# Splitting the 512-column product matmuls of a hybrid decoder layer into two of 256 columns

## The chip, the cores and the metric

One core of a Trainium2 chip runs the whole kernel. The metric is the device time of one execution in microseconds (us). Three runs of the kernel before took 1301.55, 1302.9 and 1303.37 us; the median is 1302.9 us.

## What is computed

One decoder layer over 1024 positions of width 1024, in float32. A single projection of the normed input feeds two branches, a chunked state-space scan (Mamba-2) and an attention with a forget gate; their outputs are projected, gated, added and projected again:

```python
def _hybrid_layer(x, ...):
    h = _rmsnorm(x, pre_g)
    proj = jnp.einsum('bld,de->ble', h, w_in)          # 1024 -> 9248 columns
    z_ssm, xbc, dt_raw, q, k, v, f_raw, z_att, g_ssm, g_att = jnp.split(proj, ...)
    xbc = jax.nn.silu(_causal_dwconv(xbc, conv_w, conv_b))
    y = _ssd_chunked(...)                              # 16 heads of 64, chunks of 128
    ...                                                # gate by silu(z_ssm), group norm
    o = _forgetting_attention(heads(q), heads(k), heads(v), log_f)
    y_att = o * jax.nn.silu(z_att)
    p_ssm = jnp.einsum('ble,ed->bld', y_ssm, w_branch_ssm)
    p_att = jnp.einsum('ble,ed->bld', y_att, w_branch_att)
    merged = jax.nn.sigmoid(g_ssm) * p_ssm + jax.nn.sigmoid(g_att) * p_att
    out = jnp.einsum('bld,de->ble', merged, w_out)
    return x + _rmsnorm(out, post_g)
```

## The kernel before

All the large matrix products (the projection, the two branch projections and the output projection) go through one class, `Pair`. A pair holds two blocks of 128 output columns, and multiplies them with the 1024 positions by a scheme of seven products in place of eight: the sums of the weight blocks (`total`, line 357) are made on VectorE or GpSimd, the sums of the other operand are made once for many pairs, and each of the seven products covers 512 of the 1024 inputs and 512 positions. There are 48 pairs, so 336 products.

Each number is held as a high part and a low part of a reduced float32 type (`fp32r` in the profile's forms of the writers, f32 in those of the readers). `Pair.split` (lines 351 and 352) makes both parts of the weights in the tile `wop`, one on ScalarE and one on VectorE; the other operand's parts are the tiles x0h, x0l to x6h, x6l. A product is the sum of three part products, high by high, high by low and low by high, over four blocks of 128 inputs (`KH` = 4): twelve matmuls of 128 weight columns by 512 positions (`HALF` = 512), in `Pair.matmuls`. They accumulate in one bank of PSUM, and are recorded through the helper `mm`, so that all of them have line 130 in the profile. The bank's tile is called pb, pc or pd.

`Pair.do` says which products go to which bank. Products 1, 2 and 5 open a bank (`first` is true, and the first of their twelve matmuls clears it); products 6, 7, 4 and 3 go on adding to a bank that is open. After a product the bank is copied out by `keep` (ScalarE, line 404, tile s) or combined with an earlier copy by `give` (lines 412 to 418, tiles th, u and others).

`Stream` holds the list of all products in the order in which they are done. A call of `half` issues half a product (six matmuls, up to the `yield`), and the code of the branches calls it between its own steps: the scan (`ssd`), attention (`scores`, `turned`, `weighted`), the norms. So TensorE's program alternates between pieces of products and pieces of the branches, and TensorE's order is written by hand (`mm` and `turn` keep the program order). Other instructions that are not pinned are put in order by the scheduler, which goes by a simulated clock of its own.

Attention works on pairs of heads. Its scores (tile s) are matmuls of 64 rows, two of them side by side on the two halves of the array, over 128 to 512 positions, with the high and low parts of the same reduced type. ScalarE's exponential (line 1468, tile ex) follows, then transposes by TensorE (`turn`, line 133, tile pt), a copy (line 1499, tile p), and the weighting of the values (tile av). Eight pairs of heads with six groups each make 48 groups, and in each group two stretches of products are issued (`fill`), one after the scores and one after the transposes.

Of the kernel before, what the change touches and what calls it, by code (L numbers as in the profile page):

```python
# [20 lines left out]
KH = NK // 2  # L21
NT = T // P
HALF = 512
# [63 lines left out]
def hybrid_layer(ctx: ExitStack, tc, a, out):  # L87
# [41 lines left out]
    def mm(*args, **kw):  # L129
        return tc.keep_in_program_order(nc.tensor.matmul(*args, **kw))  # L130
# [191 lines left out]
    class Pair:  # L322
# [65 lines left out]
        def matmuls(self, ps, which, x, first):  # L388

            op = self.op.pop(which)  # L390
            xh, xl = self.ops[x]
            for k in range(KH):
                if k == KH // 2:
                    yield
                for n, (w, m) in enumerate(((0, xh), (0, xl), (1, xh))):
                    mm(
                        ps, op[:, w, k, :], m[:, k, :], start=first and k == 0 and n == 0,
                        stop=k == KH - 1 and n == 2, skip_group_check=True,
                    )

        def keep(self, ps):
            s = wp.tile([P, HALF], F32, tag="s", bufs=3, name="s")
# [890 lines left out]
    with tc.tile_pool(name="att", bufs=1, reuse_waits="tile", side="right") as ap, tc.tile_pool(  # L1293
# [24 lines left out]
        q, k, v, fb = {}, {}, {}, {}  # L1318
# [408 lines left out]
```

## Time and profile before

| | |
|---|---|
| median of three runs | 1302.9 us |
| profiled execution, first to last instruction (the only time that its page gives) | 1304.1 us |
| TensorE matmuls | 7054, busy 1259.0 us |
| TensorE weight loads | 7054, busy 984.6 us |
| VectorE | busy 1009.6 us |
| ScalarE | busy 791.9 us |
| GpSimd | busy 263.9 us |
| mean granted TensorE clock | 0.996 |
| HBM traffic | 180 GB/s over the span |

In the profile's rows PE is TensorE's matmul part and PEld its weight loads; DVE is VectorE, ACT is ScalarE, POOL is GpSimd, SP is the engine whose queue issues most transfers. A row of the timeline has the start, the length, the engine, the line of the kernel, the operation, the tile written and the tiles read, the shapes, and how many neighbouring instructions it stands for. Matmuls overlap: the length of one is longer than the distance to the next, and the ends are modelled. A row of groups has the count, then the busy time and the mean length of one in ns, then the idle time before it with what ended that.

### The profile page before, as it was taken

What the parts mean: (1) busy time and instruction counts of PE and PEld (TensorE: products, weight loads), DVE (VectorE), ACT (ScalarE), POOL (GpSimd) and SP (SyncE); (2) the same over time, 40 slices, a digit from 0 to 9 for tenths busy, and PEclk for the clock granted to TensorE, in tenths of its full rate; (3) what the DMA queues carried; (4) which work ended last, traced back from release to release, by engine and by line L of the source; (5) the groups of instructions that cost most, each with busy time, mean ns of one, the idle gap of its engine ahead of it and who ended that gap; (6) DMA issues with size and microseconds to landing.
All of it is one profiled execution on the core that took longest, in us unless ns stands there. A gap on an engine that the chain in (4) does not pass through costs nothing.

```text
span 1304.1 us, 20960 instructions
## 1 busy us (share of the span) xinstructions
PE 1259.0 (97%) x7054; PEld 984.6 (76%) x7054; DVE 1009.6 (77%) x1994; ACT 791.9 (61%) x1738; POOL 263.9 (20%) x250
## 2 busy tenths in 40 slices
PE   5999999999999999999999999999999999899997
PEld 4678878777888888788877777777667777678886
DVE  7989986887888888898767566666787676686975
ACT  7745665456665666567545666666675657653754
POOL 3000440013400340124101021120001002146052
PEclk9999999999999999999999999999999999899999
DMA  8222543555436543654365575666866658556933
GB/s 294 76 107 75 164 143 100 161 170 172 130 110 199 175 145 96 209 164 137 114 207 198 183 227 190 225 211 217 281 206 241 211 194 295 190 170 201 364 107 104
DMA packets 153515, 233.57 MB, mean 179 GB/s; under 512 B 15968, under 2 KB 61504, under 8 KB 153408
## 3 DMA queue, kind: packets, MB, share of 16 engines
q1 hardware_dynamic: 142016, 205.53, 49.4%
q0 software_dynamic: 4864, 15.99, 3.1%
q10 hardware_dynamic: 6528, 10.72, 2.2%
q8 instruction: 55, 0.90, 0.3%
q14 instruction: 52, 0.43, 0.1%
HBM read 162.99 MB, written 72.34 MB: 180 GB/s over the span
## 4 chain that ended last, share of the span: by engine, by line
PE 66%; DVE 12%; ACT 8%; DMA 7%; issue 4%; POOL 1%; SPq 1%; ACTq 0%; DVEq 0%; POOLq 0%
PE pb L130 27%; PE pc L130 16%; PE av L130 5%; PE pd L130 4%; PE pt L133 4%; PE s L130 4%; ACT ex L1468 2%; DVE wop L352 2%; PE yps L130 2%; DMA raw<-in_wu 1%; DMA qh_dram<-th 1%; DVE sum L357 1%; ACT wop L351 1%; DMA xt<-in_x 1%; DVE ex L1464 1%
## 5 line engine op out<-in xcount | busy, mean ns | idle before, releaser
L1468 ACT ACTIVATE ex<-ex,nm 128x512 f32<-128x512 f32 (+1 forms) x192 | 116.0, 606 | 131.1 <-DVE nm L1464 129.7
L352 DVE TENSOR_TENSOR wop<-sum,wop 128x512 fp32r<-128x512 f32 x180 | 138.2, 768 | 57.3 <-ACT wop L351 55.8
L351 ACT ACTIVATE wop<-sum 128x512 fp32r<-128x512 f32 x180 | 112.3, 625 | 80.1 <-DVE sum L357 34.1
L404 ACT ACTIVATE s<-pb 128x512 f32<-128x512 f32 x144 | 85.0, 590 | 88.7 <-PE pb L130 85.8
L352 DVE TENSOR_TENSOR wop<-raw,wop 128x512 fp32r<-128x512 f32 x144 | 105.2, 732 | 42.7 <-ACT wop L351 41.4
L130 PE MATMUL pc<-x3h,wop 128*128 128x512 f32 x384 | 131.4, 400 | 4.1 <-DVE th L418 2.8
L130 PE MATMUL pc<-x2h,wop 128*128 128x512 f32 x384 | 130.6, 399 | 2.4 <-DVE th L416 1.9
L130 PE MATMUL pb<-x0h,wop 128*128 128x512 f32 x384 | 131.3, 399 | 0.0
L130 PE MATMUL pb<-x6h,wop 128*128 128x512 f32 x384 | 129.3, 395 | 1.3 <-ACT s L404 1.3
L130 PE MATMUL pb<-x5h,wop 128*128 128x512 f32 x384 | 129.3, 395 | 1.0 <-ACT s L404 1.0
L130 PE MATMUL pb<-x4h,wop 128*128 128x512 f32 x384 | 129.4, 395 | 0.0
L1464 DVE CUSTOM_DVE_ANT_0 ex<-s,fb 128x512 f32<-128x512 f32 (+1 forms) x192 | 95.7, 552 | 36.0 <-PE s L130 36.0
L351 ACT ACTIVATE wop<-raw 128x512 fp32r<-128x512 f32 x144 | 89.6, 623 | 13.7 <-PE pc L130 5.8
L130 PE MATMUL pd<-x1h,wop 128*128 128x512 f32 x288 | 96.3, 394 | 0.0
L130 PEld LDWEIGHTS pc<-x3h,wop 128*128 128x128 f32 x384 | 72.6, 189 | 23.0 <-issue 4.1
L130 PEld LDWEIGHTS pc<-x2h,wop 128*128 128x128 f32 x384 | 72.1, 188 | 20.7 <-DVE th L416 3.3
L130 PEld LDWEIGHTS pb<-x5h,wop 128*128 128x128 f32 x384 | 72.1, 188 | 18.3 <-ACT s L404 1.8
L130 PEld LDWEIGHTS pb<-x6h,wop 128*128 128x128 f32 x384 | 72.2, 188 | 17.8 <-ACT s L404 2.1
L130 PEld LDWEIGHTS pb<-x0h,wop 128*128 128x128 f32 x384 | 72.7, 189 | 16.2 <-issue 0.9
L133 PE MATMUL pt<-ident,ex 128*128 128x128 f32 x576 | 76.9, 277 | 7.9 <-ACT ex L1468 7.5
L130 PEld LDWEIGHTS pb<-x4h,wop 128*128 128x128 f32 x384 | 72.1, 188 | 16.0 <-issue 0.9
L133 PEld LDWEIGHTS pt<-ident,ex 128*128 128x128 f32 x576 | 65.9, 142 | 19.8 <-ACT ex L1468 13.8
(310 smaller groups left out, 2921.6 us busy)
## 6 DMA issues: line engine op xcount, KB each, us to landing
raw<-in_wu SPq DMA_DIRECT2D x128, 256.0 KB
csb<-cs_dram SPq DMA_DIRECT2D x32, 256.0 KB
fb<-f_dram SPq DMA_DIRECT2D x16, 512.0 KB
rb<-st_dram SPq DMA_DIRECT2D x48, 128.0 KB
wd<-in_wo SPq DMA_DIRECT2D x40, 128.0 KB
xt<-in_x SPq DMA_DIRECT2D x8, 512.0 KB
gs_dram<-th ACTq DMA_DIRECT2D x16, 256.0 KB
qh_dram<-th SPq DMA_DIRECT2D x16, 256.0 KB
```

Source lines behind the costliest of these rows:

```text
L130: return tc.keep_in_program_order(nc.tensor.matmul(*args, **kw))
L133: return tc.keep_in_program_order(nc.tensor.transpose(out_, in_, idn))
L351: nc.scalar.activation(op[:, 0], src, AF.Copy)
L352: nc.vector.tensor_tensor(op[:, 1], src, op[:, 0], ALU.subtract)
L357: self.adds.tensor_tensor(t, x, y, ALU.add)
L404: nc.scalar.activation(s, ps, AF.Copy)
L1464: nc.vector.tensor_tensor_reduce(o, s[e][:, 0:w], fb[hp, h][:, e, 0:w], 1.0, 3.0e38, ALU.add, ALU.min, nm)
L1468: pin(nc.scalar.activation(o, o, AF.Exp, scale=-1.0, bias=nm, accum_out=hd.at(hd.sm, i, h, e)))
```

## The change

In `Pair.matmuls`, only the matmul that opens a bank keeps its 512 columns. Every other one is issued as two, for the columns 0 to 255 and 256 to 511 of the same bank, with the same weights. The flags stay as they were; the flag that ends a product is now on both halves of its last matmul.

```diff
                 for n, (w, m) in enumerate(((0, xh), (0, xl), (1, xh))):
-                    mm(
-                        ps, op[:, w, k, :], m[:, k, :], start=first and k == 0 and n == 0,
-                        stop=k == KH - 1 and n == 2, skip_group_check=True,
-                    )
+                    begin = first and k == 0 and n == 0
+
+                    for cols in (slice(0, HALF),) if begin else (slice(0, HALF // 2), slice(HALF // 2, HALF)):
+                        mm(
+                            ps[:, cols], op[:, w, k, :], m[:, k, cols], start=begin,
+                            stop=k == KH - 1 and n == 2, skip_group_check=True,
+                        )
```

## The prediction

> **What bounds the kernel now.** I read the page's engine totals first, then its chain, then the list of waits, then single places of the timeline.
>
> ```profile
> span 1304.1 us, 20960 instructions
> PE 1259.0 (97%) x7054; PEld 984.6 (76%) x7054; DVE 1009.6 (77%) x1994; ACT 791.9 (61%) x1738; POOL 263.9 (20%) x250
> PE 66%; DVE 12%; ACT 8%; DMA 7%; issue 4%; POOL 1%; SPq 1%; ACTq 0%; DVEq 0%; POOLq 0%
> PE pb L130 27%; PE pc L130 16%; PE av L130 5%; PE pd L130 4%; PE pt L133 4%; PE s L130 4%; ACT ex L1468 2%; DVE wop L352 2%; PE yps L130 2%; DMA raw<-in_wu 1%; DMA qh_dram<-th 1%; DVE sum L357 1%; ACT wop L351 1%; DMA xt<-in_x 1%; DVE ex L1464 1%
> ```
>
> TensorE is busy for 97% of the span, and it has one weight load for each matmul: 7054 of both. The chain that ended last runs over PE for 66%; the products (tiles pb, pc and pd) alone make up 27 + 16 + 4 = 47%. A busy share says little where matmuls overlap in the array, so the next question is whether the products really stand back to back. They do, in the merged chain, in the timeline, and in the count by window:
>
> ```profile
> 112.40 8.16 PE pb L130 x36
> 1272.58 0.39 PE L130 MATMUL pb<-x0h,wop 128*128 128x512 f32 x1
> 1272.58 0.19 PEld L130 LDWEIGHTS pb<-x0l,wop 128*128 128x128 f32 x1
> 1275.30 0.39 PE L130 MATMUL pb<-x6h,wop 128*128 128x512 f32 x1
> 0.00:700.00 700.00, 580.86 (x2466) 458.77 (x2466) 153.03 (x208) 130.12 (x209) 1.00 0.48 153
> 700.00:1140.00 440.00, 234.34 (x912) 165.05 (x912) 55.68 (x77) 47.25 (x77) 0.99 0.66 217
> 1140.00:1304.10 164.10, 150.07 (x654) 122.30 (x654) 44.84 (x51) 31.60 (x51) 0.99 0.56 189
> ```
>
> The first row gives 8.16 / 36 = 0.2267 us from one 512-column matmul to the next. The rows at 1272.58 and 1275.30 stand twelve matmuls apart: 2.72 / 12 = 0.2267 again. A matmul's own length (0.39) is longer than this, because neighbours overlap; what counts is the spacing. The load of the next matmul's weights starts when the matmul before starts (both at 1272.58) and takes 0.19, so it lies wholly beside the stream of 0.2267. The last three rows are the windows view for the tile wop alone (PE busy and count, then the loads): 2466 + 912 + 654 = 4032 product matmuls, so 4032 x 0.2267 = 914 us, or 70% of the span, are products.
>
> What TensorE waits for is little:
>
> ```profile
> PE pt L133 <- DVE rstd L1165: 8.6, 1, 8.6
> PE pt L133 <- ACT ex L1468: 7.5, 17, 1.3
> PE av L130 <- ACT p L1499: 4.5, 8, 1.2
> PE pc L130 <- DVE th L418: 3.3, 4, 1.5
> PE pb L130 <- ACT s L404: 2.3, 3, 1.3
> 1296.83 0.39 PE L130 MATMUL pb<-x6h,wop 128*128 128x512 f32 x1
> ```
>
> Idle in all is 1304.1 - 1259.0 = 45.1 us. Of it 8.6 come before the first transpose, and the last matmul ends at 1297.2, which leaves 6.9 after it. Between them 45.1 - 8.6 - 6.9 = 29.6 us are left over the whole kernel. So the kernel is bound by TensorE nearly everywhere, and a longer product is paid for nearly in full.
>
> **The change, part by part.** Of the 4032 product matmuls, the first of a bank stays whole: products 1, 2 and 5 open a bank, once for each of 48 pairs, so 144 matmuls. The other 3888 become two each: 3888 more matmuls, and as many more weight loads. The streamed columns stay the same. Will the second load really be issued, where the weights are the same as the first's? The kernel has such neighbours already: xh and xl are multiplied in turn by the same weights, and each xl matmul has a load of its own:
>
> ```profile
> L130 PE MATMUL pb<-x0l,wop 128*128 128x512 f32 x192 | 75.4, 393 | 0.0
> L130 PEld LDWEIGHTS pb<-x0l,wop 128*128 128x128 f32 x192 | 36.4, 190 | 6.8
> ```
>
> 192 matmuls and 192 loads: none is left out. Now the price of a half. No 256-column product stands in the trace; the nearest are the attention scores at 256 columns, which have the same number type for the moving side and 128 weight columns, but work on 64 rows each, two at a time in the two halves of the array:
>
> ```profile
> L130 PEld LDWEIGHTS s<-k,q 64*128 64x128 f32 x576 | 45.5, 185 | 15.3 <-issue 11.5 <-DMA fb<-f_dram 0.2 <-DMA th<-gs_dram 0.2
> 715.23 0.40 PE L130 MATMUL s<-k,q 64*128 64x256 f32 x4
> 715.35 0.28 PE L130 MATMUL s<-k,q 64*128 64x256 f32 x2
> ...
> 1141.90 0.39 PE L130 MATMUL s<-k,q 64*128 64x256 f32 x4
> 1142.02 0.28 PE L130 MATMUL s<-k,q 64*128 64x256 f32 x2
> 802.52 0.19 PEld L130 LDWEIGHTS pc<-x2h,wop 128*128 128x128 f32 x1
> 802.63 0.19 PEld L130 LDWEIGHTS pc<-x2l,wop 128*128 128x128 f32 x1
> ```
>
> From the second pair of scores to the third it is 0.12 at 715.23 and at 1141.90; these are the first and the last of 16 such places, which lie between 0.116 and 0.119 with a mean of 0.118. The last two rows are two loads of full product weights with no stream between: the second starts 0.11 after the first, though each is drawn 0.19 long. So a load holds the array for about 0.11, just under the 0.118, and still hides. I take 0.118 for a half. Two halves are 0.236 against 0.2267: 0.0093 more for each matmul that is split, and 3888 x 0.0093 = 36 us. Bounds: at 0.116 it is 0.0053 each, or 21 us; at 0.120 (a little above what the scores show, for the full-height load) it is 0.0133, or 52 us.
>
> The Trainium skill, "TensorE: Matmul & The Clock Gate", section "The mechanism" of Part 3, speaks against the change more strongly: it says that a weight load overlaps running matmuls only where it goes to another row group. By that rule each of the 3888 added loads would lie bare, at 0.11 each an estimated 428 us more. The trace disagrees already: the load at 1272.58 runs beside a matmul on the same rows.
>
> What of the 36 us is hidden? Only what falls into the 29.6 us of waits. Attention's 48 groups have two gaps each that are filled with products, and 912 products lie there: 9.5 a gap, which grow by 9.5 x 0.0093 = 0.09 us. The 25 waits on ex and p (17 and 8, of about 0.5 us each) can each swallow this much: 2.2 us. The waits on evicted sums (th and s, seven in the rows above) follow a chain of some 5 us, in which 22 products grow by 0.2 us: 1.4 us. I take 4 us hidden. Bounds: nothing, and the 29.6 whole.
>
> At no cost, with what covers it: the compiled kernels hold the same instructions on VectorE, ScalarE, GpSimd and the queues, but some neighbours change places (87 of 1996 on VectorE, 36 of 1594 on ScalarE, 19 of 874 on SP's queue, one of 252 on GpSimd), since the scheduler's own clock sees longer products. VectorE at 77% and ScalarE at 61% cover that; without the cover the waits on th and s (3.3 + 2.3) could double or go, so 6 us either way. No wait is added: the second half of the last matmul releases the bank, and the evictions queue as before. The added instructions have to be fetched and issued; the scores issue two loads and two matmuls in 0.118, twice what a half needs. The granted clock is the last term:
>
> ```profile
> 1100.00:1200.00 100.00, 93.08 (x493) 71.13 (x492) 71.55 (x141) 52.77 (x121) 36.27 (x28) 0.97 0.59 192
> ```
>
> 3% of these 100 us is a stretch at a lower clock in the last, half-empty attention groups; it may go or stay, 3 us at most.
>
> The sum: 1304.1 + 36 - 4 = 1336 for the profiled execution. Its span lies 1.2 us above the median of the three runs, so against these it is 1302.9 + 32 = 1335.
>
> **The rivals.** First, the loads stop hiding. If the whole drawn length of a load (189 ns for the products, by the rows of x0l and its like) had to pass between two starts, a half would cost 0.19 instead of 0.118: 3888 x (2 x 0.19 - 0.2267) = 596 us, so about 1900. It decides from the point where a load holds the array longer than 0.118. For it: a load of full height at the rate of a half has no example here. Against it: the scores' loads are drawn 185 ns long and follow each other every 0.118, and the product loads at 802.52 stand 0.11 apart.
>
> Second, the other side, faster: the time lost from one product matmul to the next belongs to the long stream and not to each instruction. The transposes of attention show a spacing with hardly any such time:
>
> ```profile
> 805.36 0.82 PE L133 MATMUL pt<-ident,ex 128*128 128x128 f32 x6
> L133 PE MATMUL pt<-ident,ex 128*128 128x128 f32 x576 | 76.9, 277 | 7.9 <-ACT ex L1468 7.5
> ```
>
> (0.82 - 0.277) / 5 = 0.109 for each. If a half-width product kept that beat, two would take 0.218, 0.0087 less than now: 3888 x 0.0087 = 34 us gained, so 1269. It decides from a half below 0.1134. For it: full-height matmuls with their loads do run at 0.109. Against it: those stream other data at 128 columns, and the scores, which are of the products' kind, need 0.118.
>
> Third, a small fixed time: a half costs 0.1146, so that a split costs some 2.5 ns, 10 us, and the time is 1313. For it: the scores come in pairs, and a second matmul issued beside the first may lengthen their beat, which a single product would not pay. Against it: none of the 16 places is below 0.116. The Trainium skill (same page, section "Back-to-back issue gap") gives the warm gap as the columns over 2.4 plus 2.5 ns; by it a split costs 2.5 ns and the estimate is 1313 too, but by it a 512-column matmul would take 216 ns, where the trace has 226.7.
>
> Fourth, TensorE is not the bound: the added time goes into its waits. At most 29.6 of the 36 us can, which leaves 1309; if the loads of the waiting matmuls hide there as well, no change at all is left.
>
> **How the numbers follow.** Forecast 0.86, loads bare 0.03, faster 0.04, small fixed time 0.04, hidden 0.03 (two thirds of it no change that can be measured). A measurement of this kernel tells about 0.2%, 2.6 us, from no change. That makes faster 0.04, same 0.02, slower 0.94. The range takes the bounds of the half: 1302.9 + 21 - 9 = 1315 (more hidden than I take, or a swap that helps), and 1302.9 + 52 + 3 = 1358 (nothing hidden, a stretch of low clock more). It leaves out the bare loads, the faster case, most of the hidden and the small fixed time, and some 0.06 of the forecast's own tails.
>
> **What would show it.** In the changed profile: 7054 + 3888 = 10942 matmuls and as many loads; product rows of 256 columns, with their starts 0.118 apart; stretches of twelve, now 2.72 us, that become 2.83 (twelve splits at 0.0093 more each; eleven where the stretch opens a bank); PE's share of the chain not lower than 66%; waits on ex and p a little shorter. A spacing of halves at 0.113 or less, or halves near 0.19, proves the forecast wrong at its main step. If the spacing is 0.118 and the time still stands within 3 us of before, then the waits hid it and the reading of the bound is wrong.

## The result and the profile after

The changed kernel takes 1342.5 us (median of 4 runs, 1341.96 to 1343.82) against 1303.1 us before: 39.4 us more, a ratio of 1.0295 with a 95% interval of 1.0274 to 1.0315. In a later set of runs it was 1341.5 against 1302.3, ratio 1.0307 (1.028 to 1.0334). The forecast was 1335 with a range of 1315 to 1358.

The page of the changed kernel, its span, engine totals and chain:

```profile
span 1340.3 us, 28752 instructions
PE 1300.6 (97%) x10942; PEld 1201.2 (90%) x10942; DVE 1011.2 (75%) x1994; ACT 793.8 (59%) x1738; POOL 256.6 (19%) x250
PE 76%; DVE 7%; ACT 6%; DMA 5%; issue 3%; POOL 1%; SPq 0%; ACTq 0%; DVEq 0%; POOLq 0%
PE pb L130 34%; PE pc L130 18%; PE pd L130 6%; PE av L130 4%; PE pt L133 4%; PE s L130 4%; ACT ex L1471 2%; PE yps L130 2%; DVE wop L352 1%; DMA raw<-in_wu 1%; DMA xt<-in_x 1%; PE tr L133 1%; ACT wop L351 1%; DVE ex L1467 1%; DVE sum L357 1%
```

TensorE has 10942 matmuls and as many loads, 3888 more of each. PE's share of the span stays at 97%, but that of the loads goes from 76% to 90%. PE's share of the chain goes up by ten points, and VectorE, ScalarE and the transfers lose nine between them: more of the chain now runs over TensorE. VectorE's busy time, 1011.2 us after 1009.6, has hardly moved, so its share falls with the longer span.

Now the beat of the products (the time from one start to the next): a long stretch of the merged chain, then a place in the timeline, then groups of one operand, the last of them from the trace before (a group's columns after the count are busy us, the mean length in ns, and the idle time before it):

```profile
69.29 8.63 PE pb L130 x71
```

```profile
115.20 0.64 PE L130 MATMUL pb<-x5h,wop 128*128 128x256 f32 x4
115.68 0.40 PE L130 MATMUL pb<-x5l,wop 128*128 128x256 f32 x2
115.92 0.64 PE L130 MATMUL pb<-x5h,wop 128*128 128x256 f32 x4
115.81 0.55 PEld L130 LDWEIGHTS pb<-x5h,wop 128*128 128x128 f32 x4
```

```profile
L130 PE MATMUL pc<-x2h,wop 128*128 128x256 f32 x768 | 134.6, 286 | 1.5 <-DVE th L419 1.3
L130 PEld LDWEIGHTS pc<-x2h,wop 128*128 128x128 f32 x768 | 109.1, 191 | 4.0 <-DVE th L419 1.9
```

```profile
L130 PEld LDWEIGHTS pc<-x2h,wop 128*128 128x128 f32 x384 | 72.1, 188 | 20.7 <-DVE th L416 3.3 <-issue 1.4 <-DVE u L416 0.8
```

Six halves fill the 0.72 us from 115.20 to 115.92: 0.120 each. The stretch of 71 is one opening matmul and 70 halves: 70 x 0.120 + 0.227 = 8.63. So a split matmul takes 0.240 where it took 0.2267. Over 3888 splits that is 51.7 us. The load path hardly rests any more: ahead of the 384 loads of x2h it was idle 20.7 us in all before, and ahead of the 768 of now it is idle 4.0 us.

Of these 51.7 us, 36.2 arrive in the two spans and 39.4 in the medians (the profiled execution of before was one of the slower ones). The waits of TensorE show a part of the rest:

```profile
PE pt L133 <- ACT ex L1471: 6.1, 15, 1.3
PE av L130 <- ACT p L1502: 4.8, 9, 1.0
PE pb L130 <- ACT s L407: 1.7, 2, 1.0
PE pc L130 <- DVE th L421: 0.8, 1, 0.8
```

The idle time of PE falls from 45.1 to 1340.3 - 1300.6 = 39.7 us. All start times of the two traces, set side by side, divide the 15.5 us that are missing between the spans. Delays of over 0.14 us beyond the beat, between one product matmul and the next, fall from 14.22 to 6.66 us in all (7.6 us). Waits among the transposes and other matmuls fall by 2.5 us. One half in five starts 0.116 to 0.118 and not 0.120 after its forerunner (4 us), and small irregularities get rarer (1.4 us).

### The profile page after: what moved, and what is told of

It reads as the page before. It is cut to its first block, busy times and chain, and to the rows that moved or that the text cites. A ratio compares the mean times of both kernels' runs of the same rounds, so it can differ in the third digit from the quotient of the medians.

```text
span 1340.3 us, 28752 instructions
## 1 busy us (share of the span) xinstructions
PE 1300.6 (97%) x10942; PEld 1201.2 (90%) x10942; DVE 1011.2 (75%) x1994; ACT 793.8 (59%) x1738; POOL 256.6 (19%) x250
## 4 chain that ended last, share of the span: by engine, by line
PE 76%; DVE 7%; ACT 6%; DMA 5%; issue 3%; POOL 1%; SPq 0%; ACTq 0%; DVEq 0%; POOLq 0%
PE pb L130 34%; PE pc L130 18%; PE pd L130 6%; PE av L130 4%; PE pt L133 4%; PE s L130 4%; ACT ex L1471 2%; PE yps L130 2%; DVE wop L352 1%; DMA raw<-in_wu 1%; DMA xt<-in_x 1%; PE tr L133 1%; ACT wop L351 1%; DVE ex L1467 1%; DVE sum L357 1%
## 5 line engine op out<-in xcount | busy, mean ns | idle before, releaser
L130 PE MATMUL pc<-x3h,wop 128*128 128x256 f32 (+1 forms) x720 | 135.1, 295 | 1.5 <-DVE th L421 0.8
L130 PE MATMUL pc<-x2h,wop 128*128 128x256 f32 x768 | 134.6, 286 | 1.5 <-DVE th L419 1.3
L130 PE MATMUL pb<-x0h,wop 128*128 128x256 f32 (+1 forms) x720 | 135.5, 295 | 0.0
L130 PE MATMUL pb<-x6h,wop 128*128 128x256 f32 x768 | 133.8, 285 | 1.0 <-ACT s L407 1.0
L130 PE MATMUL pb<-x5h,wop 128*128 128x256 f32 x768 | 133.7, 285 | 0.7 <-ACT s L407 0.7
L130 PE MATMUL pb<-x4h,wop 128*128 128x256 f32 x768 | 134.0, 285 | 0.0
L130 PEld LDWEIGHTS pb<-x6h,wop 128*128 128x128 f32 x768 | 109.7, 191 | 2.7 <-ACT s L407 1.4
L130 PEld LDWEIGHTS pb<-x4h,wop 128*128 128x128 f32 x768 | 109.5, 191 | 1.4 <-issue 0.9
L130 PE MATMUL pd<-x1h,wop 128*128 128x256 f32 (+1 forms) x540 | 99.6, 292 | 0.0
L130 PEld LDWEIGHTS pd<-x1h,wop 128*128 128x128 f32 x540 | 77.6, 190 | 3.5 <-issue 2.5
```

## The experiments

The forecast had two terms: what a split costs, and how much of it the waits swallow. The theories on the first:

- **Theory 1**: each matmul pays for its columns and a fixed time beside (13.3 ns, by 0.2267 and 0.120). This is the forecast's view.
- **Theory 2**: a half waits for its weight load; the 0.120 is the load's.

**Other widths.** Each operand is cut in its own way.

```diff
+WIDTHS = {
+    "b11": (0, 256, 512), "b21": (0, 384, 512), "-b22": (0, 448, 512), "t1": (0, 320, 512),
+    "-t2": (0, 128, 256, 384, 512), "t3": (0, 288, 512), "t4": (0, 512),
+}
 ...
-                    for cols in (slice(0, HALF),) if begin else (slice(0, HALF // 2), slice(HALF // 2, HALF)):
+                    edges = (0, HALF) if begin else WIDTHS[x]
+                    for lo, hi in zip(edges, edges[1:]):
+                        cols = slice(lo, hi)
```

> Each product is cut in its own way: x0 at 256, x1 at 384, x2 at 448, x3 at 320, x5 at 288, x4 into four of 128, x6 not at all. Theory 1 (every matmul pays its columns, 0.417 ns each, and a fixed 13.3 ns; that is what 0.2267 and 0.1200 for 512 and 256 columns give): starts 0.200 apart after 448 columns, 0.173 after 384, 0.147 after 320, 0.133 after 288, 0.107 after 224, 0.093 after 192, 0.067 after 128, 0.040 after 64; time about 1355. Theory 2 (the 0.120 of a half is the beat of the weight loads): the wide parts as in theory 1, but every part of 256 columns or fewer at 0.117 to 0.120; a pair of halves is then a lucky cut, the uneven ones cost up to 0.09 each, and the time is about 1303 + 250 = 1550.

Measured: 1521.7 us against 1303.4. In the timeline, the cut at 448 (x2), and then the quarters (x4) in the merged chain:

```profile
277.69 0.48 PE L134 MATMUL pc<-x2h,wop 128*128 128x448 f32 x2
278.00 0.48 PE L134 MATMUL pc<-x2l,wop 128*128 128x448 f32 x2
278.31 0.79 PE L134 MATMUL pc<-x2h,wop 128*128 128x448 f32 x4
278.94 0.45 PE L134 MATMUL pc<-x2l,wop 128*128 128x448 f32 x1
```

```profile
144.31 5.36 PE pb L134 x48
```

Four matmuls cut at 448 fill 1.25 us, 0.313 each; 48 quarters fill 5.36 us, 0.112 each. A part of 64 columns thus costs as much as one of 128. The medians of the starts, for one matmul of 512 columns that is cut:

| cut | 512 | 256 + 256 | 288 + 224 | 320 + 192 | 384 + 128 | 448 + 64 | 4 x 128 |
|---|---|---|---|---|---|---|---|
| us | 0.227 | 0.240 | 0.243 | 0.258 | 0.286 | 0.313 | 0.444 |

Theory 1 alone (0.240 for every cut in two) is dead. The narrow part costs what a load costs, about 0.111, and the sum of the wide part (at the 0.443 ns a column of 0.2267 for 512) and 0.111 meets each of the four uneven cuts within 6 ns. It misses the even cut by 16 ns: 0.113 + 0.111 is 0.224, not 0.240. Theory 2 holds for the narrow parts, but its figure was wrong: loads can follow each other every 0.111, below the 0.120 of a half. So this run leaves open what the 0.120 is. Single starts are not used here, only sums over a period: the gap after the 448 columns reads 0.284 and the one after the 64 reads 0.029. I take it that a matmul which waits for its load is drawn as started early.

**Other neighbours.** The part products are put in another order, so that three neighbours add to the same columns and few neighbours share their weights. (The expectation says that none do, but where one column half ends and the other begins, xl and xh still stand side by side on the high part of the weights: one neighbouring pair in six, where the changed kernel has four in six.)

```diff
-                for n, (w, m) in enumerate(((0, xh), (0, xl), (1, xh))):
-                    for cols in ...:                                 # shortened
+                for cols in (slice(0, HALF // 2), slice(HALF // 2, HALF)):
+                    for n, (w, m) in enumerate(((0, xh), (1, xh), (0, xl))):
 ...
```

> The same matmuls of 256 columns as the changed kernel, but the three part products of one column half come before the other half, with the two high-by-high and high-by-low ones apart, so that no two neighbours share their weights and three neighbours add to the same columns. Theories 1 and 2: spacing 0.120 as before, time as the changed kernel, 1342 within 4. Rival (the second half's load is cheaper because the weights stand there already, or neighbours on other columns of the bank are cheaper): spacing above 0.120, each ns worth 7.8 us.

Measured: 1343.2 us, the median spacing 0.120 for every operand. The stretch of three products in the merged chain is as long as in the changed kernel:

```profile
69.04 8.63 PE pb L130 x71
```

The rival is dead: far fewer loads find their weights there already, and nothing gets dearer. Such a load is neither skipped nor cheaper.

**Lighter loads.** Some operands load 64 of the 128 weight columns.

```diff
+HALVES, FOUR, WHOLE = (0, 256, 512), (0, 128, 256, 384, 512), (0, 512)
+SHAPES = {
+    "b11": (HALVES, 64), "b21": (FOUR, 64), "-b22": (FOUR, 128), "t1": (HALVES, 128),
+    "-t2": ((0, 448, 512), 64), "t3": (WHOLE, 64), "t4": (WHOLE, 128),
+}
 ...
-                            ps[:, cols], op[:, w, k, :], m[:, k, cols], start=begin,
+                            ps[0:wide, cols], op[:, w, k, 0:wide], m[:, k, cols], start=begin,
```

> After the run with many widths two things are left apart: a matmul pays its columns and a fixed 13.3 ns, and no matmul comes sooner than 0.111 after the one before. If the second is the beat of a load of 128 weight columns, it must fall with the weight columns. Here some products load only 64 of their 128 weight columns and so leave out half of their output rows: x0 in halves and x1 in quarters with 64, x4 cut at 448 with 64, x5 whole with 64; x2 in quarters and x3 in halves with all 128, x6 whole. Theory (stream plus 13.3 ns, or the load): with 64 weight columns 0.120 for halves, 0.067 for quarters, 0.200 + 0.058 for the cut at 448, 0.2267 whole; with 128, 0.120 and 0.111. Rival A (a floor of every matmul, whatever its load): quarters with 64 stay at 0.111. Rival B (the 0.120 of a half hangs on its load too): halves with 64 fall below 0.120.

The time, 1445.3 us against 1304.5, mixes all these cuts; the beats tell more. Three neighbouring pieces of the merged chain, quarters with 128 weight columns (pc), quarters with 64 behind one opening matmul (pd), and the cut at 448 with 64 (the last row):

```profile
80.27 5.31 PE pc L135 x48
85.58 2.92 PE pd L135 x45
88.50 3.09 PE pb L135 x24
```

5.31 / 48 = 0.111 and (2.92 - 0.23) / 44 = 0.061 (the median of the starts is 0.060). The twelve matmuls cut at 448 take 3.09 / 12 = 0.26 each (0.262 by the median of the starts; 0.258 was expected), where they took 0.313 with 128 weight columns. Halves with 64 weight columns stand 0.113 apart at the median, halves with 128 stand at 0.120; whole matmuls are at 0.229 with 64 and at 0.228 with 128. Rival A is dead, and rival B holds: the 0.120 of a half hangs on its load. Two halves at 0.113 take 0.226, the time of a whole one. So the forecast's picture of the price, a fixed time of 9 to 13 ns for each instruction, was wrong: from 128 to 512 columns a matmul with a light load takes some 0.44 to 0.47 ns a column (0.060, 0.113 and 0.229) and little beside.

**Operands of 2 bytes.** Weights and moving columns of some products are both read as bf16.

```diff
+KINDS = {
+    "b11": (HALVES, True), "b21": (WHOLE, True), "-b22": (FOUR, True), "t1": (HALVES, False),
+    "-t2": (WHOLE, False), "t3": (FOUR, True), "t4": (WHOLE, True),
+}
 ...
+                        lhs, rhs = op[:, w, k, :], m[:, k, :]
+                        if cast:
+                            lhs, rhs = (t.bitcast(BF16).rearrange("p (c two) -> p c two", two=2)[:, :, 1] for t in (lhs, rhs))
```

> Is the fixed 13.3 ns a matter of the loads of 4-byte weights? x0 in halves, x1 and x6 whole, x2 and x5 in quarters read only the upper two bytes of each number as bf16 (low parts of the products are lost); x3 in halves and x4 whole stay as they are. Theory (fixed time of any matmul, load apart): bf16 at 0.120 for halves, 0.2267 whole, and 0.067 for quarters, since the short loads of bf16 weights (0.1 long where the masks of attention use them) no longer bind. Rival: the 13.3 ns come from the 4-byte load, and bf16 stands at 0.107, 0.213 and 0.053 with some 2 ns more. A third outcome, slower bf16 streams, would come from reading every second 2-byte element.

Measured, medians of the starts: halves 0.113, quarters 0.057, whole 0.225; the 4-byte halves beside them 0.120. Neither prediction hit the halves (0.120 by the one, 0.107 and some 2 ns by the other). It is the same picture as with 64 weight columns, by another way of making a load light: a bf16 load is drawn 97 ns long in this trace, one of 64 4-byte columns 134 ns in the run before, one of 128 4-byte columns 189 to 192 ns. Each way changes something else too: 64 weight columns halve the output rows, and bf16 halves the bytes of the moving columns. The lighter load is what the two have in common. The time, 1324.2 us against 1304.5, says little on the price, since x3 still pays for its halves and the changes between 2-byte and 4-byte products may cost something; this run doesn't settle how much. Its trace has 94 loads whose matmul isn't recorded (11566 loads, 11472 matmuls), 48 of them right behind the opening matmul of x1, so the gaps of 0.47 to 0.56 us there cover two matmuls. It also shows how far drawn starts can be trusted: each of the 28 4-byte matmuls that directly follow a whole bf16 one is drawn 0.026 or 0.027 us after it, though the stream of that takes 0.225.

**The change with light loads, all of it.** The decisive pair: both kernels use 64 weight columns everywhere but at the opening matmul; one has whole matmuls, the other the change's halves.

```diff
-                    for cols in (slice(0, HALF),) if begin else (slice(0, HALF // 2), slice(HALF // 2, HALF)):
+                    edges, wide = ((0, HALF), P) if begin else ((0, HALF), P // 2)             # whole
+                    edges, wide = ((0, HALF), P) if begin else ((0, HALF // 2, HALF), P // 2)  # halves
```

> All product matmuls but the one that opens a bank use only 64 of their 128 weight columns (the other half of the output rows is left out), at 512 columns: the kernel before with light loads. Every theory: spacing 0.224 to 0.227, time as before, 1303 within 5.

> The same light loads (64 weight columns, the other half of the output rows left out), with the split of the change: 3888 more matmuls and loads, as in the changed kernel. Theory (the changed kernel's halves wait for their weight loads; a matmul itself costs 0.443 ns a column and next to nothing beside): halves at 0.113, two of them 0.226, so nothing is paid for the split: within 5 us of the run with whole matmuls and light loads. The forecast's theory (each further instruction costs a fixed 9 to 13 ns): +28 to +40 against that run.

Measured, 10 runs each: 1308.9 us whole (1304.8 to 1311.0) and 1309.8 us in halves (1307.8 to 1314.0), against 1303.6 before; ratios to before of 1.0038 (1.0019 to 1.0057) and 1.0049 (1.0033 to 1.0066). The two differ by 0.9 us, as the theory says; the forecast's +28 to +40 is out. The expectation for the whole matmuls is missed a little: they take 5 to 6 us more than before, just over the 5 that were allowed, and stand at 0.230, not at 0.224 to 0.227. Why whole matmuls with 64 weight columns take some 2 to 3 ns longer stays open. From the pages and the merged chains, whole first:

```profile
PE 1262.9 (97%) x7054; PEld 779.3 (60%) x7054; DVE 1011.2 (78%) x1994; ACT 792.4 (61%) x1738; POOL 261.7 (20%) x250
69.07 8.28 PE pb L130 x36
```

```profile
PE 1257.8 (96%) x10942; PEld 1142.4 (87%) x10942; DVE 1009.4 (77%) x1994; ACT 790.6 (60%) x1738; POOL 263.2 (20%) x250
68.82 8.19 PE pb L130 x71
```

Both have the same work; the second has the change's 3888 further matmuls and loads, and its PE is busy no longer than the first's. The three products of this stretch take 8.28 us whole and 8.19 in halves; the changed kernel took 8.63 for them, and such a stretch of the kernel before took 8.16. So 3888 further matmuls and loads cost nothing that can be measured once the loads are light, and the price of the split is what the loads of 128 4-byte weight columns add to a half. This pair alone would leave another reading, that the halved output rows matter and not the load; the bf16 halves, which write all 128 rows and stand at 0.113 too, speak against it.

**How the load enters.** Halves everywhere, with 80 to 128 weight columns.

```diff
+COLUMNS = {"b11": 96, "b21": 112, "-b22": 104, "t1": 128, "-t2": 120, "t3": 80, "t4": 124}
 ...
+                    edges, wide = ((0, HALF), P) if begin else ((0, HALF // 2, HALF), COLUMNS[x])
```

> Halves everywhere, with a number of weight columns for each operand (what lies beyond is left out of the output): x5 80, x0 96, x2 104, x1 112, x4 120, x6 124, x3 128. If the load is what a half waits for: 0.113 as long as the load is the shorter, then a rise of 0.83 ns a column up to 0.120 at 128, so the bend lies near 120 columns. If 128 is special: 0.113 up to 124 and 0.120 at 128.

| weight columns | 64 (earlier run) | 80 | 96 | 104 | 112 | 120 | 124 | 128 |
|---|---|---|---|---|---|---|---|---|
| median from start to start, us | 0.113 | 0.114 | 0.117 | 0.118 | 0.117 | 0.118 | 0.118 | 0.120 |

The time is 1323.2 us (one run) against 1303.6. Neither expectation fits: there is no bend near 120 columns, and 128 does not stand alone above the rest. The spacing leaves 0.113 between 64 and 96 columns, and then climbs slowly, in steps of 1 to 3 ns, where the trace counts whole ns. So the load does not simply take over where it is the longer (128 columns can be loaded every 0.111, below the 0.113 of the stream); it already lengthens the beat where it comes near the stream. How it does so stays open.

**Where the rest went.** Three kernels split only some products, to see what arrives in the time. The first splits inside attention's loop only, the second everywhere else, the third only the high-by-low matmul of each three.

```diff
+                    whole = begin or not (inside["att"])   # first
+                    whole = begin or not (not inside["att"])   # second
+                    whole = begin or n != 1   # third
+                    for cols in (slice(0, HALF),) if whole else (slice(0, HALF // 2), slice(HALF // 2, HALF)):
```

> Only the products issued inside attention's loop are split: 902 splits, 12.0 us at 0.0133 each. The prediction's step (waits in attention swallow 2 us): +10, 1313. Reading of the lag between the two traces (only half of it arrives there): +6.5, 1309.5.

> All products but those issued inside attention's loop are split: 2986 splits, 39.7 us at 0.0133 each. The prediction's step (1.4 us of waits on evicted sums hidden): +38, 1341. Reading of the lag between the two traces (three quarters of it arrive outside attention): +30, 1333. If the two stages add up, this and the run that splits inside attention alone give the 39.4 of the whole change.

> Only the high-by-low matmul of each three is split: 1344 splits, 17.9 us at 0.0133 each, spread evenly over the kernel. If the hidden share is the same at any dose (a quarter): +13.6, 1316.5, a third of the whole change. If a fixed reserve of some 10 us of waits is used up first: +8, 1311. If nothing is hidden: +18, 1321.

> The changed kernel once more, on the same chip as the three partial ones, so that they can be set against it: +39 against before.

Measured on one chip, before at 1302.3:

| split | splits | at 13.3 ns | time | more than before | ratio, 95% interval |
|---|---|---|---|---|---|
| inside attention | 902 | 12.0 | 1309.8 | 7.5 | 1.0055, 1.0034 to 1.0076 |
| elsewhere | 2986 | 39.7 | 1335.9 | 33.6 | 1.025, 1.0228 to 1.0271 |
| high by low | 1344 | 17.9 | 1317.6 | 15.3 | 1.0112, 1.0089 to 1.0135 |
| all (the change) | 3888 | 51.7 | 1341.5 | 39.2 | 1.0307, 1.028 to 1.0334 |

Inside attention 7.5 of 12.0 us arrive (4.4 to 9.9 by the interval: the forecast's +10 lies at its upper end, the +6.5 from the traces inside). Elsewhere 33.6 of 39.7 arrive (29.7 to 35.3: +30 is inside, +38 is not). The two add to 41.1, the whole change on this chip is 39.2; so the stages add up within what can be told. By the medians more than a third of a split's price is hidden inside attention and about a sixth elsewhere, though the two intervals overlap. The split of each third matmul brings 15.3 of 17.9 (11.6 to 17.6); a fixed reserve used up first (+8) is out, nothing hidden (+18) lies just outside, and the even share (+13.6) is in. The changed kernel itself came as expected (+39).

## Why the prediction came out as it did

**The bound.** Right. The products' beat decided: PE's part of the chain went from 66% to 76%.

**The added loads.** Right: 10942 loads, none left out for weights that were there.

**The price of a half: wrong by the size and by the cause.** I took 0.118 from the scores, between bounds of 0.116 and 0.120; it is 0.120, the upper bound, and a split costs 0.0133 instead of 0.0093: 51.7 us instead of 36. The step that failed is the sentence that a load "holds the array for about 0.11, just under the 0.118, and still hides". It does not hide wholly: with 64 weight columns the same half takes 0.113, and the price of the split is gone (1308.9 and 1309.8). The scores could not show this, since their own loads have 128 columns of 4 bytes too; I read their 0.118 as a matter of the matmul.

**The rivals.** The faster one was half right: the time of a matmul goes by its columns and not by each instruction, since two halves with light loads take 0.226. But even they win back nothing against a whole one (0.2267), so the 0.218 of that rival did not come with light loads either. The row that I took it from, the transposes at 0.109 for 128 columns, did not show a lean stream: quarters of 128 columns stand at 0.111 with 128 4-byte weight columns and at 0.060 with 64, so such a beat can be that of the load. (No run took the transposes themselves apart.) What lengthens a half is the load, which is the first rival's mechanism in a mild form: it does not add 0.07 to a half, but 0.007. The small fixed time of 2.5 ns (1313) and the hidden case (1309) did not come. The Trainium skill's rule on row groups ("TensorE: Matmul & The Clock Gate", section "The mechanism") would have laid each added load bare, some 0.11 for each; the same section makes an exception for loads into a background weight buffer. The runs show 0.0133 for a split, so loads for the same rows do run beside a matmul.

**What the waits hide: too small.** I took 4 us; by the medians 51.7 - 39.4 = 12 us did not arrive, by the two spans 15.5. Of the 15.5, about 10 us are waits that went (7.6 between products and 2.5 elsewhere), and 4 us come from halves that stand at 0.116 to 0.118. Inside attention, where I had 2.2 us, the run with that part alone leaves out 4.5 (2.1 to 7.6); elsewhere, where I had 1.4 us on seven waits with 0.2 each, 6.1 (4.4 to 10.0) do not arrive. There single stalls went whole: two of 1.7 and 1.1 us between products, at 540.7 and 681.0 us of the trace before, have no counterpart after. The two errors have opposite signs: +15.5 at the price and -8 at the cover leave 39.4 where 32 stood. That the forecast came within 7 us is in part luck.

**The parts at no cost.** The places that the scheduler swapped and the clock (0.996 before, 0.997 after) show no cost. No run took them apart from the rest.

**The signs named.** The counts came as told. The twelve-step stretches did become longer, but by 0.16 instead of 0.11 (70 x 0.120 + 0.227 over three products is 2.88 each). Waits on ex fell from 7.5 to 6.1 us; those on p did not (4.5 and 4.8).

## What to carry to other kernels

Before a matmul is cut, look at both beats: its own stream and the load of its weights. In these runs a cut was free where the load of each part stayed well below its stream (64 weight columns beside 256 streamed ones). With 128 columns of 4-byte weights, 256 streamed columns were already too close, and each part narrower than that cost about a full load of 0.111 us. A neighbouring row can give the size of a price and still hide its cause: a row that shares the same load cannot tell the load from the matmul.

## What the hardware showed that I had not expected

- Products of 4-byte weights: whole 0.2267 us for 512 columns, halves 0.120, quarters 0.111. With 64 weight columns: 0.229, 0.113, 0.060. With bf16 of the same shapes: 0.225, 0.113, 0.057.
- The load lengthens a half's beat from 96 weight columns on (0.117), though quarters show that even 128 columns can be loaded every 0.111.
- The matmuls stand no closer or further apart for finding their weights loaded already: 0.120 whether four neighbouring pairs in six share their weights or one.
- Drawn starts can be early: a pair that takes 0.313 shows gaps of 0.284 and 0.029, and a 4-byte matmul is drawn 0.026 after a bf16 one that streams for 0.225.
